# A fourth block unit in the second MLP's down projection, and an earlier first difference in the last stage

## The chip, the cores and the metric

The kernel runs on one core of one Trainium2 chip. The metric is the device time of one execution in microseconds (us): the median of three runs. A profile of one more execution gives the trace that the text reads.

## What is computed

Two layers of a causal decoder trunk over 512 tokens of width 1024, all in float32. Each layer is a mixer (layer 0: windowed attention beside a short convolution; layer 1: gated linear attention), a gated MLP with a width-3 convolution, and a gated per-layer embedding. The change lies in the last two pieces of layer 1:

```python
def _conv_ffn(h, w_up, conv_w, conv_b, w_down):
    u = _causal_depthwise_conv(h @ w_up, conv_w) + conv_b
    gate, up = jnp.split(u, 2, axis=-1)
    return (jax.nn.gelu(gate, approximate=False) * up) @ w_down       # 512x2816 @ 2816x1024

def _per_layer_embedding(x, p_i, norm, w_gate, w_proj):
    gate = jax.nn.sigmoid(_rms_norm(x, norm) @ w_gate)                # 512x1024 @ 1024x1024
    return gate * (p_i @ w_proj)                                      # 512x256  @ 256x1024
...
        x = x + _conv_ffn(_rms_norm(x, ffn_norm[i]), ...)
        x = x + _per_layer_embedding(x, p[i], ...)
```

## The kernel before

**Numbers in halves.** Every float32 operand of a large matmul is split into a rounded high half (written by ScalarE, ACT) and the rest (a subtraction on VectorE, DVE). A product is then three matmuls on TensorE (PE): high x high, high x low, low x high (`mm3`, L162 to L164). x lies transposed in SBUF as eight feature tiles `xT[0]` to `xT[7]`, each 128 features x 512 tokens.

**Seven block products.** Some matrix products are cut into 2 x 2 blocks and done by seven products of half-size blocks in place of eight (a Strassen-Winograd scheme). The function `seven` is a generator: it issues the products of 256 columns (L879 to L881), yields between groups of them so that the caller can put plain matmuls of 512 columns in between, and copies partial sums between PSUM banks on ACT (L890, L891, L900, L904). `first_forms`, `more_forms` and `cut_blocks` make the sums and differences of the weight blocks on DVE (L850, L851, L858, L861) and split them (L826 on ACT, L827 on DVE).

**The down stage** (`down`, one for each of the two MLPs, `i` = 0 and 1). The 1024 output features are four units `u` of two tiles each; the 2816 rows of the weight are three groups: B (rows of tiles 0 to 7), A (8 to 13), C (14 to 21). `plan` lists the steps in the order in which PE takes them: (unit, group, first row tile, last row tile, and for some steps the unit whose C rows are done by seven block products between the row tiles of this step). A plain row tile of a step is six matmuls of 512 columns. In the first MLP (`i == 0`) all four units have their C rows done by blocks (`blocked` is 4). In the second (`i == 1`) units 0 to 2 have, and unit 3's C rows are two plain steps, `(3, "C", 0, 4)` and `(3, "C", 4, 8)`. `loads` and `inner` list the weight blocks in the order of their loads: through the two buffers `raw` (L1135), or, for `inner`, into two tiles `zt` (L1144). `todo` and `pump` issue the cuts and sums a few steps ahead; `settled` adds a finished unit into x (L1193, and L1256 for the shared seventh part) and calls `finish` for its two tiles, once no block unit is left and the unit's last part is in.

**Finishing a tile in the second MLP** (`blocks`, L293 to L312): scale by the norm's gain into a scratch tile from the same pool of two `zt` tiles (`half`), split into halves (`split`, L109 and L110), sums and differences of 256 columns for the last stage's own block scheme (L308 to L312), and squares summed into `acc` (L284, L285). `e1` is the part of an even tile's first 256 tokens; `s1`, `s2`, ... are block sums.

**The last stage** (`ple1`). The 1024 x 1024 gate weight is four blocks b11, b12, b21, b22 of 512 x 512. `add` runs the products of one x form with one weight form (L1482 to L1484), `chunk` splits half a block (L1461 on ACT, L1462 on DVE) into `wh`/`wl` buffers (three each) or into a `four` tile (seven in the pool), `minus` is a difference of blocks (L1471). The first products are `e1` with b11; then `s1` with b12 - b11, the norm's merge (`end_norm`, transposes of `acc`, L329), the transposes of p (`load_p`, L1287), and so on. At the end x is turned back and written out.

**What sets the order.** A scheduler orders each engine's instructions by priority (`high_priority`), except where `manual_schedule` fixes the program order for the named engines: PE in `down`, and PE, DVE and ACT in `ple1`. Each engine takes its queue in order; loads are issued in order by SyncE (SP), and a load whose buffer is not free holds up the loads behind it.

Of the kernel before, what the change touches and what calls it, by code (L numbers as in the profile page):

```python
# [56 lines left out]
class Kernel:  # L57
# [46 lines left out]
    def split(self, hl, src, gain=None):  # L104

        nc = self.nc
        h, l = hl
        if gain is None:
            nc.scalar.activation(h, src, AF.Copy)  # L109
            nc.vector.tensor_tensor(l, src, h.bitcast(F32), ALU.subtract)  # L110
        else:
            nc.scalar.activation(h, src, AF.Copy, scale=gain)
            nc.vector.scalar_tensor_tensor(
                out=l, in0=src, scalar=gain, in1=h.bitcast(F32), op0=ALU.mult, op1=ALU.subtract
            )

    def weights(self, src, na, nb, by="b"):
        raw = self.raw(na, nb)
# [168 lines left out]
    def blocks(self, m, gain, scratch, tags):  # L287


        nc = self.nc  # L290
        H = S // 2
        gx = scratch()
        nc.scalar.activation(gx, self.xT[m], AF.Copy, scale=gain[:, m : m + 1])  # L293

        def parts(x):
            w = x.shape[1]
            h, l = self.pair(self.fp, *tags)
            self.split((h[:, :w], l[:, :w]), x)
            return lambda b, c: (h[:, b * H + c * P : b * H + (c + 1) * P], l[:, b * H + c * P : b * H + (c + 1) * P])

        if m % 2 == 0:
            self.even = gx
            self.e1 = parts(gx[:, :H])
        else:
            e, o = self.even, gx
            op = parts(o)
            s12, s34 = scratch(), scratch()
            nc.vector.tensor_tensor(s12[:, :H], e[:, H:], o[:, H:], ALU.add)  # L308
            nc.vector.tensor_tensor(s12[:, H:], s12[:, :H], e[:, :H], ALU.subtract)
            s12p = parts(s12)  # L310
            nc.vector.tensor_tensor(s34[:, :H], e[:, :H], e[:, H:], ALU.subtract)
            nc.vector.tensor_tensor(s34[:, H:], o[:, :H], s12[:, H:], ALU.subtract)  # L312
            s34p = parts(s34)
            e1 = self.e1
            at = lambda f, b: lambda c: f(b, c)
            self.forms.append(
                dict(e1=at(e1, 0), o1=at(op, 0), o2=at(op, 1), s1=at(s12p, 0), s2=at(s12p, 1), s3=at(s34p, 0),
                     s4=at(s34p, 1))
            )
        self.squares(m)  # L320
# [779 lines left out]
    def down(self, i, acts, forms, both, work, finish):  # L1100
# [7 lines left out]
        plan = [(0, "B", 0, 4), (0, "B", 4, 8), (0, "A", 0, 3), (0, "A", 3, 6)]  # L1108
        plan += [(1, "A", 0, 3), (1, "A", 3, 6), (1, "B", 0, 4), (1, "B", 4, 8, 0)]
        plan += [(2, "B", 0, 4, 1), (2, "B", 4, 8, 2)]  # L1110
        if i == 0:
            plan += [(2, "A", 0, 4, 3), (2, "A", 4, 6), (3, "B", 0, 4), (3, "B", 4, 8), (3, "A", 0, 3), (3, "A", 3, 6)]
            loads = ["B0", "A0", "A1", "B1", "C0", "B2", "C2", "A2", "B3", "A3"]
            inner = ["C1", "C3"]
        else:
            plan += [(2, "A", 0, 3), (2, "A", 3, 6), (3, "B", 0, 4), (3, "B", 4, 8)]
            plan += [(3, "C", 0, 4), (3, "C", 4, 8), (3, "A", 0, 3), (3, "A", 3, 6)]
            loads = ["B0", "A0", "A1", "B1", "C0", "B2", "C2", "A2", "B3", "C3", "A3"]
            inner = ["C1"]
        blocked = 4 - i  # L1120
        plan = [p if len(p) == 5 else p + (None,) for p in plan]
        got, cuts, gens, pending = {}, {}, {}, []

# [76 lines left out]
        with tc.manual_schedule(engines={ET.PE}):  # L1200
# [4 lines left out]
            for t, (u, name, k0, k1, s) in enumerate(plan):  # L1205
# [1 line left out]
                if own:  # L1207
                    banks[u] = [self.ps(), self.ps()]
                ends = t + 1 == len(plan) or plan[t + 1][0] != u
                joined = i == 0 and u == 3  # L1210

                def steps(lo, hi):
                    for k in range(lo, hi):
# [17 lines left out]
                if s is None:  # L1231
                    steps(0, k1 - k0)
                    settled(ends)
                    pump(1)
                    pend()
                    if work:
                        work.pop(0)()
                        if not work:
                            load_inner(inner.pop(0))
                else:  # L1240
                    g = gens[s]
                    steps(0, 1)
# [12 lines left out]
                    x = self.xT[2 * s + 1].rearrange("p (u t) -> p u t", u=2)  # L1255
                    nc.vector.tensor_tensor(x, x, V.unsqueeze(1).to_broadcast([P, 2, H]), ALU.add)  # L1256
                    if i == 0 and s == 3:
                        banks[3] = [X, Y]
                    else:
                        add(2 * s, X)  # L1260
                        add(2 * s + 1, Y)
                    pend()
                    due[s] -= 1
                    block_left -= 1
                    settled(False)
# [5 lines left out]
            self.nc.sync.dma_start(pin[e], src[:, :, e * P : (e + 1) * P])  # L1271
        return pin

    def load_p(self, i, pool, pin=None):

        nc = self.nc
        given = pin is not None
# [6 lines left out]
        for e in range(2):  # L1284
            ps = self.pa()
            for t in range(NT):
                nc.tensor.transpose(ps[:, t * P : (t + 1) * P], pin[e][:, t, :], self.ident)  # L1287
            hl = (four[:, 2 * e], four[:, 2 * e + 1]) if given else self.pair(pool, f"ph{e}", f"pl{e}")
            self.split(hl, ps)
            out.append(hl)  # L1290
        return out

    def ple0(self, fp):

# [141 lines left out]
    def ple1(self, fp):  # L1436
# [15 lines left out]
        count = [0]  # L1452

        def chunk(src):
            if count[0] % 6 < 3:
                h, l = (self.wide(g).rearrange("p (a b) -> p a b", b=H) for g in ("wh", "wl"))
            else:
                four = self.four(fp)
                h, l = four[:, :2], four[:, 2:]
# [70 lines left out]

        b11 = block(0, 0, True)
        w11 = chunks(b11)
        b12 = block(0, 1, True)
        pin = self.p_halves(1)
        b22 = block(1, 1, False)
        wj_raw = self.four(fp, F32)
        proj_load(1)
        b21 = block(1, 0, False)
        proj_load(0)
        with tc.high_priority(offset=150):  # L1540
            minus(b11, b12, b11)
            wt1 = [chunk(b11[:, :2, :])]
        X, Q = [[self.ps() for _ in range(2)] for _ in range(2)]
        both = (0, H)
        with tc.manual_schedule(engines={ET.PE, ET.DVE, ET.Activation}):
            add(X, "e1", w11, first=True)
            wt1.append(chunk(b11[:, 2:, :]))
            minus(b11, b22, b11)
            steps = [(j, i, both, Q[i]) for j in range(J) for i in range(2)]
            add(None, "s1", wt1, first=True, order=steps[:2])  # L1550

            self.end_norm()
            ka = [self.sp.tile([P, S], F32, tag="acc", name=self.nm("keep"), bufs=1), self.sq()]
            for k, x in zip(ka, X):
                nc.scalar.copy(k, x)
            wt2 = chunks(b11)
            pT = self.load_p(1, fp, pin)
            add(None, "s1", wt1, order=steps[2:])
            minus(b12, b22, b12, (0,))
            wj = chunk(wj_raw[:, 2:, :])  # L1560
            kd = keep(Q, "R")
# [521 lines left out]
```

## Time and profile before

| | us |
|---|---|
| three runs: median (lowest to highest) | 1204.29 (1204.18 to 1205.54) |
| the profiled execution's own time | 1203.80 |
| its span, from the first to the last instruction | 1202.0 |
| PE busy | 1194.0 |
| DVE busy | 989.3 |
| ACT busy | 681.1 |
| GpSimd busy | 43.7 |

A row of the timeline gives the start in us from the span's start, the duration, the engine, the line of the kernel, the operation, output<-input by the program's names and the shape. What stands in brackets at its end is the idle time of the engine just before and who ended it. The duration of a matmul includes its way through the array, which overlaps the next ones; the time that a matmul costs is the distance from its start to the next one's. A row of the windows view gives the stretch, its length, and the busy time of PE, weight loads (PEld), DVE, ACT and GpSimd (POOL), the granted clock of PE, the share of the DMA engines and GB/s. A row of the DMA view gives the tile and the tensor, the queue, the count, the size and the us from issue to landing. The granted clock of PE is 1.00 in every stretch.

### The profile page before, as it was taken

To read this page: it belongs to the slowest core of one execution; us is meant where nothing else is said; L and a number is where in the kernel's file an instruction comes from. 1 tells how busy PE (TensorE), PEld (TensorE's weight loads), DVE (VectorE), ACT (ScalarE), POOL (GpSimd) and SP (SyncE) were. 2 spreads that over 40 slices of the span, in tenths; PEclk is the share of its full clock that TensorE was granted. 3 is DMA by queue.
4 is the path that set the end of the run, shared out by engine and by line. 5 is a ranking of instruction groups with operands and counts; after the bars stand their busy time and mean duration, and the time that the engine had idled before them with its cause. 6 is when DMAs were issued, how large, how long until landed. Compare 5 with 4: busy or idle time off the path is not lost.

```text
span 1202.0 us, 17888 instructions
## 1 busy us (share of the span) xinstructions
PE 1194.0 (99%) x7085; PEld 1037.6 (86%) x7085; DVE 989.3 (82%) x1563; ACT 681.1 (57%) x1109; POOL 43.7 (4%) x64
## 2 busy tenths in 40 slices
PE   9999999999999999999999999999999999999998
PEld 8877788999899889888988988889999999888887
DVE  6786587899999996789769876677999999978595
ACT  7466465656555744566563555565555656645374
POOL 2600000000000000000100000000000000000000
PEclk9999999999999999999999999999999999999999
DMA  7221322323233342232422222313242423322501
GB/s 222 90 88 39 97 79 70 129 83 119 92 104 107 107 139 97 97 106 63 140 66 69 71 71 70 106 54 122 71 140 71 139 72 128 127 88 97 210 1 70
DMA packets 110839, 117.61 MB, mean 98 GB/s; under 512 B 2808, under 2 KB 105778, under 8 KB 110756
## 3 DMA queue, kind: packets, MB, share of 16 engines
q1 hardware_dynamic: 109920, 115.88, 29.7%
q8 instruction: 55, 0.90, 0.3%
q0 software_dynamic: 560, 0.42, 0.3%
q10 hardware_dynamic: 276, 0.18, 0.1%
q14 instruction: 28, 0.23, 0.1%
HBM read 114.37 MB, written 2.10 MB: 97 GB/s over the span
## 4 chain that ended last, share of the span: by engine, by line
PE 89%; DVE 6%; ACT 2%; issue 1%; POOL 1%; DMA 0%; SPq 0%; DVEq 0%; ACTq 0%; POOLq 0%
PE ps L162 11%; PE ps L163 11%; PE ps L164 11%; PE pa L163 7%; PE pa L162 7%; PE pa L164 7%; PE ps L879 6%; PE ps L881 6%; PE ps L880 6%; PE pa L879 2%; PE pa L881 2%; PE pa L880 2%; DVE wl L143 1%; PE ps L1484 1%; PE ps L1483 1%
## 5 line engine op out<-in xcount | busy, mean ns | idle before, releaser
L142 ACT ACTIVATE wh<-raw 128x1024 fp32r<-128x1024 f32 (+4 forms) x146 | 145.8, 999 | 124.5 <-PE ps L163 78.8
L143 DVE TENSOR_TENSOR wl<-raw,wh 128x1024 fp32r<-128x1024 f32 (+4 forms) x146 | 168.1, 1151 | 40.7 <-ACT wh L142 39.9
L826 ACT ACTIVATE wh<-raw 128x1024 fp32r<-128x1024 f32 x84 | 89.2, 1062 | 120.6 <-DVE raw L851 65.1
L939 DVE SCALAR_TENSOR_TENSOR zt<-z,vfa,zt 128x510 f32<-128x510 f32 (+1 forms) x176 | 130.6, 744 | 5.3 <-ACT zt L937 4.7
L827 DVE TENSOR_TENSOR wl<-raw,wh 128x1024 fp32r<-128x1024 f32 x84 | 102.6, 1221 | 21.3 <-ACT wh L826 21.2
L937 ACT ACTIVATE zt<-z,vfb 128x512 f32<-128x512 f32 x88 | 71.0, 810 | 21.5 <-DVE four L990 8.3
L162 PE MATMUL ps<-b,wh 128*128 128x512 f32 x192 | 76.8, 400 | 0.0
L163 PE MATMUL ps<-b,wh 128*128 128x512 f32 x192 | 75.1, 391 | 0.0
L164 PE MATMUL ps<-b,wl 128*128 128x512 f32 x192 | 75.0, 391 | 0.0
L879 PE MATMUL ps<-four,wh 128*128 128x256 f32 x248 | 69.4, 280 | 0.7 <-ACT ps L904 0.7
L163 PE MATMUL pa<-a,wh 128*128 128x512 f32 x176 | 69.0, 392 | 0.0
L163 PE MATMUL pa<-b,wh 128*128 128x512 f32 x176 | 69.0, 392 | 0.0
L162 PE MATMUL pa<-a,wh 128*128 128x512 f32 x176 | 69.0, 392 | 0.0
L162 PE MATMUL pa<-b,wh 128*128 128x512 f32 x176 | 69.0, 392 | 0.0
L881 PE MATMUL ps<-four,wl 128*128 128x256 f32 x248 | 68.8, 277 | 0.0
L880 PE MATMUL ps<-four,wh 128*128 128x256 f32 x248 | 68.6, 277 | 0.0
L164 PE MATMUL pa<-a,wl 128*128 128x512 f32 x176 | 68.4, 389 | 0.0
L164 PE MATMUL pa<-b,wl 128*128 128x512 f32 x176 | 68.4, 389 | 0.0
L162 PE MATMUL ps<-a,wh 128*128 128x512 f32 x128 | 50.6, 395 | 0.0
L162 PE MATMUL ps<-uh,wh 128*128 128x512 f32 x128 | 50.3, 393 | 0.0
L163 PE MATMUL ps<-a,wh 128*128 128x512 f32 x128 | 50.2, 392 | 0.0
L163 PE MATMUL ps<-ul,wh 128*128 128x512 f32 x128 | 50.1, 391 | 0.0
(488 smaller groups left out, 3577.4 us busy)
## 6 DMA issues: line engine op xcount, KB each, us to landing
raw<-in_ffn_w_up_dram SPq DMA_DIRECT2D x44, 1024.0 KB, 5.0
raw<-in_ffn_w_down_dram SPq DMA_DIRECT2D x13, 1024.0 KB, 4.8
raw<-in_hy_w_in_dram SPq DMA_DIRECT2D x8, 1024.0 KB, 5.1
raw<-in_gla_w_in_dram SPq DMA_DIRECT2D x8, 1024.0 KB, 5.2
raw<-in_ffn_w_down_dram SPq DMA_DIRECT2D x8, 768.0 KB, 4.2
raw<-in_ple_w_gate_dram SPq DMA_DIRECT2D x6, 1024.0 KB, 4.8
raw<-in_hy_w_out_dram SPq DMA_DIRECT2D x16, 256.0 KB, 4.0
raw<-in_gla_w_out_dram SPq DMA_DIRECT2D x4, 1024.0 KB, 4.8
```

The costliest lines, as they stand in the source:

```text
L142: nc.scalar.activation(hv, v, AF.Copy)
L143: nc.vector.tensor_tensor(lv, v, hv.bitcast(F32), ALU.subtract)
L162: mm(out, lh, rh, start=start, stop=False, **kw)
L163: mm(out, lh, rl, start=False, stop=False, **kw)
L164: mm(out, ll, rh, start=False, stop=stop, **kw)
L826: nc.scalar.activation(h, src, AF.Copy)
L827: nc.vector.tensor_tensor(l, src, h.bitcast(F32), ALU.subtract)
L879: mm(out, wh, xh, start=first and j == 0, stop=False, **kw)
L880: mm(out, wh, xl, start=False, stop=False, **kw)
L881: mm(out, wl, xh, start=False, stop=j == ND // 2 - 1, **kw)
L937: nc.scalar.activation(y, z, AF.Identity, scale=w2[:, f : f + 1], bias=bb[:, f : f + 1])
L939: nc.vector.scalar_tensor_tensor(out=y[:, tap:], in0=z[:, : S - tap], scalar=w[:, f : f + 1], in1=y[:, tap:], op0=ALU.mult, op1=ALU.add,)
```

## The change

In the second MLP the plan, the loads and `blocked` become those of the first: unit 3's C rows are done by seven block products within the step `(2, "A", 0, 4, 3)`, their weight block is loaded in two parts into `zt` tiles, and the two PSUM banks of that product are the ones into which unit 3's B and A rows are then summed. Unit 3 now ends with the A rows as before, but without the two plain C steps.

In the last stage:

- b12 is loaded into a `four` tile and b21 into a `raw` buffer (before: the other way round), so b12's load does not wait for a `raw` buffer.
- The first difference b12 - b11 is made in two halves with the split of the first half between them. The split of the second half is held (`issue_after`) behind the split of `e1` of x's seventh tile (`xT[6]`).
- `chunk` gives the third split a `four` tile and the fourth a `wh`/`wl` pair (before: the other way round).
- Within the `s1` products, the transposes of p and the split of the first half of the next form (`wt2`, the old difference taken from b22) come after two steps, then three more steps, then the norm's merge and the copies of `e1`'s sums, then the second half of `wt2` and the last three steps. The low halves of p (`rests`) follow after all of them. Before, the merge, the copies, both halves of `wt2` and p with its low halves all came after two steps.

```diff
@@ def split @@
-            nc.scalar.activation(h, src, AF.Copy)
-            nc.vector.tensor_tensor(l, src, h.bitcast(F32), ALU.subtract)
+            first = nc.scalar.activation(h, src, AF.Copy)
+            second = nc.vector.tensor_tensor(l, src, h.bitcast(F32), ALU.subtract)
...
+        return first, second
@@ def blocks @@
-            self.split((h[:, :w], l[:, :w]), x)
+            self.halves = self.split((h[:, :w], l[:, :w]), x)
...
             self.e1 = parts(gx[:, :H])
+            self.e1_split = self.halves
@@ def down @@
-        if i == 0:
-            plan += [(2, "A", 0, 4, 3), (2, "A", 4, 6), (3, "B", 0, 4), (3, "B", 4, 8), (3, "A", 0, 3), (3, "A", 3, 6)]
-            loads = ["B0", "A0", "A1", "B1", "C0", "B2", "C2", "A2", "B3", "A3"]
-            inner = ["C1", "C3"]
-        else:
-            plan += [(2, "A", 0, 3), (2, "A", 3, 6), (3, "B", 0, 4), (3, "B", 4, 8)]
-            plan += [(3, "C", 0, 4), (3, "C", 4, 8), (3, "A", 0, 3), (3, "A", 3, 6)]
-            loads = ["B0", "A0", "A1", "B1", "C0", "B2", "C2", "A2", "B3", "C3", "A3"]
-            inner = ["C1"]
-        blocked = 4 - i
+        plan += [(2, "A", 0, 4, 3), (2, "A", 4, 6), (3, "B", 0, 4), (3, "B", 4, 8), (3, "A", 0, 3), (3, "A", 3, 6)]
+        loads = ["B0", "A0", "A1", "B1", "C0", "B2", "C2", "A2", "B3", "A3"]
+        inner = ["C1", "C3"]
+        blocked = 4
...
-                joined = i == 0 and u == 3
+                joined = u == 3
...
-                    if i == 0 and s == 3:
+                    if s == 3:
                         banks[3] = [X, Y]
@@ def load_p @@
-            self.split(hl, ps)
-            out.append(hl)
-        return out
+            nc.scalar.activation(hl[0], ps, AF.Copy)
+            out.append((hl, ps))
+
+        def rests():
+            for (h, l), ps in out:
+                nc.vector.tensor_tensor(l, ps, h.bitcast(F32), ALU.subtract)
+
+        if not later:
+            rests()
+        hls = [hl for hl, _ in out]
+        return (hls, rests) if later else hls
@@ def ple1 @@
-            if count[0] % 6 < 3:
+            if count[0] % 6 < 3 and count[0] != 2 or count[0] == 3:
...
-        b12 = block(0, 1, True)
+        b12 = block(0, 1, False)
...
-        b21 = block(1, 0, False)
+        b21 = block(1, 0, True)
         proj_load(0)
+        rounded, rest = (x.ins for x in self.e1_split)
         with tc.high_priority(offset=150):
-            minus(b11, b12, b11)
+            minus(b11, b12, b11, (0,))
             wt1 = [chunk(b11[:, :2, :])]
+            minus(b11, b12, b11, (1,))
...
             add(X, "e1", w11, first=True)
-            wt1.append(chunk(b11[:, 2:, :]))
+            with tc.issue_after(rounded), tc.issue_after(rest):
+                wt1.append(chunk(b11[:, 2:, :]))
             minus(b11, b22, b11)
             steps = [(j, i, both, Q[i]) for j in range(J) for i in range(2)]
             add(None, "s1", wt1, first=True, order=steps[:2])
-
+            pT, rests = self.load_p(1, fp, pin, True)
+            wt2 = [chunk(b11[:, :2, :])]
+            add(None, "s1", wt1, order=steps[2:5])
             self.end_norm()
             ...
-            wt2 = chunks(b11)
-            pT = self.load_p(1, fp, pin)
-            add(None, "s1", wt1, order=steps[2:])
+            wt2.append(chunk(b11[:, 2:, :]))
+            add(None, "s1", wt1, order=steps[5:])
+            rests()
```

More of the change, by code (lines that the diff above doesn't have):

```diff
@@ L108, in split @@
         if gain is None:
-            nc.scalar.activation(h, src, AF.Copy)
-            nc.vector.tensor_tensor(l, src, h.bitcast(F32), ALU.subtract)
-        else:
-            nc.scalar.activation(h, src, AF.Copy, scale=gain)
-            nc.vector.scalar_tensor_tensor(
+            first = nc.scalar.activation(h, src, AF.Copy)
+            second = nc.vector.tensor_tensor(l, src, h.bitcast(F32), ALU.subtract)
+        else:
+            first = nc.scalar.activation(h, src, AF.Copy, scale=gain)
+            second = nc.vector.scalar_tensor_tensor(
                 out=l, in0=src, scalar=gain, in1=h.bitcast(F32), op0=ALU.mult, op1=ALU.subtract
             )
+        return first, second
     def weights(self, src, na, nb, by="b"):
@@ L1272, in p_halves, with load_p @@
         return pin
-    def load_p(self, i, pool, pin=None):
+    def load_p(self, i, pool, pin=None, later=False):
         nc = self.nc
```

## The prediction

> **What bounds the kernel now.** I read the page first: the share of each engine, then the chain that ended last.
>
> ```profile
> PE 1194.0 (99%) x7085; PEld 1037.6 (86%) x7085; DVE 989.3 (82%) x1563; ACT 681.1 (57%) x1109; POOL 43.7 (4%) x64
> ...
> PE 89%; DVE 6%; ACT 2%; issue 1%; POOL 1%; DMA 0%; SPq 0%; DVEq 0%; ACTq 0%; POOLq 0%
> ```
>
> TensorE (PE) is busy almost from end to end and the chain is made of it. A busy share says little, since matmuls overlap, so what counts is the distance from one matmul's start to the next in the timeline: where that distance is always the same, the queue of PE never runs dry, and only fewer or shorter matmuls save time. I therefore went through the timeline of PE from the second MLP's down stage to the end, looking for starts that come later than the beat. The first MLP's down stage serves as a natural experiment: it already takes all four units by seven block products, the second one only three. Here are the first matmul of each stage and the first after it:
>
> ```profile
> 408.77 0.40 PE L162 MATMUL ps<-uh,wh 128*128 128x512 f32 x1
> ...
> 524.69 0.39 PE L162 MATMUL ps<-a,wh 128*128 128x512 f32 x1
> ...
> 1026.37 0.40 PE L162 MATMUL ps<-uh,wh 128*128 128x512 f32 x1
> ...
> 1143.44 0.39 PE L1482 MATMUL ps<-wh,b 128*128 128x512 f32 x1
> ```
>
> The stage with four such units took 524.69 - 408.77 = 115.92 us, that with three 1143.44 - 1026.37 = 117.07 us. The matmul work is otherwise the same, so 1.15 us is the first estimate of what the fourth unit brings.
>
> **The change part by part.** *The fourth unit's C rows.* Removed are 48 matmuls of 512 columns (8 row tiles x 2 feature tiles x 3 products of halves); this is their place, from the first of them to the first of the next step:
>
> ```profile
> 1124.40 0.39 PE L162 MATMUL ps<-four,wh 128*128 128x512 f32 x1
> ...
> 1135.28 0.39 PE L162 MATMUL ps<-four,wh 128*128 128x512 f32 x1
> ```
>
> That is 10.88 us, or 0.2267 us each. Added are 84 of 256 columns (7 products x 4 x 3); the order of the changed kernel's PE queue indeed has 36 instructions more, so the change does what it says. Their price is in the first MLP, where the same 84 lie between the four plain steps of the unit before:
>
> ```profile
> 487.75 0.40 PE L162 MATMUL ps<-four,wh 128*128 128x512 f32 x1
> ...
> 489.14 0.28 PE L879 MATMUL pa<-four,wh 128*128 128x256 f32 x1
> ...
> 490.52 0.40 PE L162 MATMUL ps<-four,wh 128*128 128x512 f32 x1
> ...
> 502.90 0.40 PE L162 MATMUL ps<-four,wh 128*128 128x512 f32 x1
> ```
>
> The whole run of four steps and seven products took 502.90 - 487.75 = 15.15 us. The four steps are 24 matmuls of 512 columns, 24 x 0.2267 = 5.44 us, which leaves 9.71 us for the 84, their changes of width included. The first product alone, 12 matmuls, took 490.52 - 489.14 = 1.38 us, 0.115 us each, so nothing waited there. Against 10.88 us this saves 1.17 us, in line with the 1.15 us of the whole stages.
>
> A product of the seven can still wait for the copy or the split ahead of it. The three units of the second MLP show how much; this is the worst place of the third:
>
> ```profile
> 1102.11 0.39 PE L164 MATMUL ps<-uh,wl 128*128 128x512 f32 x1
> 1102.44 0.38 PE L879 MATMUL ps<-b,wh 128*128 128x256 f32 x1
> 1102.66 0.28 PE L880 MATMUL ps<-b,wh 128*128 128x256 f32 x1
> ```
>
> The starts are 0.33 and 0.22 us apart instead of 0.23 and 0.11: 0.21 us lost, because the norm's squares and splits stand ahead of the copy in ACT's queue. The change holds that norm work back until the fourth unit, so this loss can move there or vanish here. Bounds: from 0.21 us given back to 0.21 us gained beside the 1.17. I take zero, nearest to the first MLP's fourth unit, which lost nothing.
>
> *What this adds elsewhere.* In blocks the unit needs on DVE eight operations of 512 and two of 1024 elements a row, in place of two of 1024; on ACT four copies of 256, three splits of 512 and two of 1024, in place of two of 1024. The paces of DVE, start to start, are in four neighbouring rows:
>
> ```profile
> 1106.47 0.42 DVE L110 TENSOR_TENSOR b<-zt,b 128x256 fp32r<-128x256 f32 x1
> 1106.81 1.22 DVE L143 TENSOR_TENSOR wl<-raw,wh 128x1024 fp32r<-128x1024 f32 x1
> 1107.95 0.68 DVE L110 TENSOR_TENSOR b<-zt,b 128x512 fp32r<-128x512 f32 x1
> 1108.55 0.42 DVE L308 TENSOR_TENSOR zt<-zt 128x256 f32<-128x256 f32 x1
> ```
>
> So 0.34 us for 256, 1.14 for 1024, 0.60 for 512, and DVE gets 8 x 0.60 = 4.8 us more. It has room in the stretch from the third unit's end to the last stage:
>
> ```profile
> 1106.60:1143.44 36.84, 36.84 (x164) 30.50 (x163) 21.79 (x31) 13.51 (x20) 0.00 (x0) 1.00 0.56 196
> ```
>
> Columns two to five are PE, weight loads, DVE and ACT: DVE is busy for 21.79 of 36.84 us. Cost: nothing on the path, as long as DVE's work keeps its order of need. If that cover is gone, each us by which DVE is late is a us of PE.
>
> *The norm's blocks come later.* The two scratch tiles that carry the fourth unit's rows are also the norm's scratch, and units 0 to 2 are finished only once no block unit is left. Before, 168 matmuls, 38 us of plain steps, lay behind that point; after, 2.72 + 10.88 + 8.16 = 21.8 us (12, 48 and 36 matmuls at 0.2267). DVE's last split for the unit, in the first MLP:
>
> ```profile
> 495.88 1.22 DVE L827 TENSOR_TENSOR wl<-zt,wh 128x1024 fp32r<-128x1024 f32 x1 [1.71 <-ACT wh L826]
> ```
>
> It ended 497.10 - 487.75 = 9.35 us into the 15.15. So from that split to the last stage PE has 15.15 - 9.35 + 21.76 = 27.6 us. In the changed kernel's DVE order I count between the two 15 operations of 256, 17 of 512, two of 768 and seven of 1024. With the 768s bounded by a 1024 this is 15 x 0.34 + 17 x 0.60 + 9 x 1.14 = 25.6 us. It fits with 2 us to spare, and the last two of them (2.3 us) are needed only some steps into the last stage. This is the thinnest cover of the change.
>
> *The last stage.* Nothing is added to or taken from PE; the eight transposes of p and the four of the norm's merge only swap places with matmuls. Moved are the first weights' difference (its first half now ahead of x's last sums) and one split behind the first norm split of x's sixth tile. What these free is seen here, first who delivers, then who needs it:
>
> ```profile
> 1146.52 0.42 DVE L110 TENSOR_TENSOR a<-zt,a 128x256 fp32r<-128x256 f32 x1
> ...
> 1149.07 0.68 DVE L285 TENSOR_TENSOR acc<-acc,sq 128x512 f32<-128x512 f32 x1
> ```
>
> ```profile
> 1147.97 0.39 PE L1484 MATMUL ps<-wh,a 128*128 128x512 f32 x1
> ...
> 1150.24 0.60 PE L329 MATMUL pa<-cf,acc 128*128 128x128 f32 x4
> ```
>
> The split ends 1146.94, 1.03 us ahead of its matmul; the sum of squares 1149.75, 0.49 us ahead of the merge. Both were already in time. Moving the merge three steps (3 x 0.68) back makes the second margin larger than 2.5 us, but a margin that grows brings no time. Gain: zero; cost: zero while the other margins stay above zero.
>
> *The loads.* The order on SP's queue changes: b12's block now goes to a tile that PE frees with the last product of the fourth unit, and b11's (the first one needed), b22, the projection, b21 and p's second half stand behind it.
>
> ```profile
> raw<-in_ple_w_gate_dram SPq DMA_DIRECT2D x2, 1024.0 KB, 5.4
> four<-in_ple_w_gate_dram SPq DMA_DIRECT2D x2, 1024.0 KB, 4.9
> ```
>
> ```profile
> 1135.25 1.06 ACT L1461 ACTIVATE wh<-raw 128x1024 fp32r<-128x1024 f32 x1 [4.59 <-PE ps L163]
> ```
>
> Even one after the other, b12 and b11 land 4.9 + 5.4 = 10.3 us after that product; the first cut of b11 waits, as in the row above, for PE to give back a weight buffer, which happens 2.72 + 10.88 = 13.6 us after it. PE still ends that wait, with 3.3 us to spare. b21 and p's second half wait for the last cut of the A rows, for which PE frees a weight buffer half-way through the B rows, 8.16 + 5.44 = 13.6 us before the last stage; if DVE's queue delays that cut by 5 us, 8 us are left, and p's half is needed 6.8 us into the stage.
>
> The sum: -1.17 +- 0.21 from the products, 0 from the rest; I take -1.15, the whole-stage comparison. Against the profiled execution that is 1203.80 - 1.15 = 1202.65 us. The median of the runs, 1204.29, lies 0.49 above it, so 1204.29 - 1.15 = 1203.1 us. What a measurement of this kernel can tell from no change is about 0.2%, 2.4 us; the forecast of -0.1% lies inside it.
>
> **The rivals.** *DVE becomes the bound.* The 25.6 us of DVE work in 27.6 us leave no room for handshakes with ACT, and each one costs. From 2.0 us of waits on (4.3 us, if the last two operations slip behind), PE stands at the last stage's first weights. With 6 us of waits in the window, PE loses about 4, and the time is 1204.29 - 1.15 + 4 = 1207.1 us. For it: that stretch has long waits of DVE for ACT, like the 1.71 us in the row of 495.88. Against: the wait there is for PE to free a buffer, before the window. I give it 0.10.
>
> *The gain is given back.* One stall of about 1.2 us in the last stage, where splits of the later weights are made just in time, and the time stays at 1204.3 us. The 0.49 us margin shows that such places exist, but it is the one that widens. 0.07.
>
> *Half-wide matmuls are bound by their weight loads.* If 84 pairs go at the mean of a weight load, 1037.6/7085 = 0.146 us, they take 12.3 us in place of 10.88, and the time is 1204.29 + 1.4 = 1205.7 us. The 0.115 us of the first MLP's product speaks against it. The Trainium skill has this rule ("TensorE: Matmul & The Clock Gate", Back-to-back issue gap): in a stream of weight load and matmul pairs both set the spacing, about 81 ns at 128 and 131 ns at 512 columns; a line between them would make 84 x 0.098 - 48 x 0.131 = +1.9 us, an estimate. This trace does not agree: 0.2267 us at 512 columns. 0.02.
>
> *More than the sum.* The small losses at the products of all four units close as the norm work leaves their queue (three times 0.2 to 0.3), and the restarts in the last stage shorten a little: some 1.2 us more, 1201.9 us, and 1201.8 with the 0.11 us by which the lowest of the three runs lies under the median. This is at the line of 0.2%, and I count it as faster. No row shows those restarts to depend on the moved work. 0.11.
>
> **How the numbers follow.** The forecast keeps 0.70. Its own range is 1202.7 to 1203.5 (the 0.21 either way and rounding). The range of 8 in 10 takes in "more" at the low end, 1201.8, and no gain at the high end with the 1.25 us by which the highest of the three runs lay above the median: 1204.3 + 1.25 = 1205.6; outside is the DVE case. Faster by over 0.2%: 0.11. Slower by over 0.2%: 0.10. Within: 0.70 + 0.07 + 0.02 = 0.79.
>
> **What would show it right or wrong.** Right: the second down stage takes 115.9 us like the first, its 84 new matmuls start 0.113 to 0.118 us apart, and the last stage from its first matmul to the end is as long as before. DVE's window behind the fourth unit would be nearly full, with no PE start off the beat at the first weights of the last stage. Wrong: a wait of PE for a split of L1462's line there (DVE is the bound), a first cut of b11 that a DMA releases, or starts 0.14 us apart in the new products.

## The result and the profile after

The changed kernel took 1203.07 us (median of 21 runs, 1202.1 to 1204.92), the kernel before 1204.61 (median of 21, 1203.98 to 1206.14). The ratio is 0.9987, with a 95% interval of 0.9981 to 0.9993: it is faster, by 0.07% to 0.19%, less than the 0.2% that the forecast took as its line. The profiled execution took 1202.58 us with a span of 1200.8 (before 1203.80 and 1202.0).

The page of the changed kernel, its busy times:

```profile
PE 1192.9 (99%) x7121; PEld 1038.1 (86%) x7121; DVE 994.2 (83%) x1571; ACT 685.2 (57%) x1116; POOL 42.9 (4%) x64
```

PE has 36 matmuls more and is busy 1.1 us less; DVE has 4.9 us more. PE remains the bound. Lines have moved: the plain matmuls are now L163 to L165, those of the products L881 to L883, those of the last stage L1486 to L1488, the merge L331.

The timeline of PE at the starts of the second down stage, of the fourth unit's step, of the step behind it and of the last stage, and the last matmul of all:

```profile
1026.32 0.40 PE L163 MATMUL ps<-uh,wh 128*128 128x512 f32 x1
...
1105.30 0.40 PE L163 MATMUL ps<-four,wh 128*128 128x512 f32 x1
...
1120.45 0.40 PE L163 MATMUL ps<-four,wh 128*128 128x512 f32 x1
...
1142.24 0.39 PE L1486 MATMUL ps<-wh,b 128*128 128x512 f32 x1
...
1196.22 0.28 PE L1488 MATMUL ps<-four,a 128*128 128x256 f32 x1
```

The stage takes 1142.24 - 1026.32 = 115.92 us, which was 117.07. The fourth unit's step takes 1120.45 - 1105.30 = 15.15 us, the same as in the first MLP. The last stage runs as long as before: 53.98 us to its last matmul (before 53.95). All of the gain that the traces show lies in the down stage. They are one execution each, with 1.2 us between their spans; the medians differ by 1.54 us, and the interval allows 0.8 to 2.3.

In the windows view, DVE's stretch from its last split for the fourth unit to the last stage (columns: length, PE, PEld, DVE, ACT, POOL, clock, DMA share, GB/s):

```profile
1114.61:1142.24 27.63, 27.63 (x142) 23.50 (x141) 25.17 (x41) 18.27 (x29) 0.00 (x0) 1.00 0.65 229
```

DVE is busy for 25.17 of 27.63 us, PE for all of it.

### The profile page after: what moved, and what is told of

It is laid out like the page before. It is cut to its first block, busy times and chain, and to the rows that moved or that the text cites. A ratio compares the mean times of both kernels' runs of the same rounds, so it can differ in the third digit from the quotient of the medians.

```text
span 1200.8 us, 17976 instructions
## 1 busy us (share of the span) xinstructions
PE 1192.9 (99%) x7121; PEld 1038.1 (86%) x7121; DVE 994.2 (83%) x1571; ACT 685.2 (57%) x1116; POOL 42.9 (4%) x64
## 4 chain that ended last, share of the span: by engine, by line
PE 89%; DVE 6%; ACT 2%; issue 1%; POOL 1%; DMA 0%; SPq 0%; ACTq 0%; DVEq 0%; POOLq 0%
PE ps L163 11%; PE ps L164 11%; PE ps L165 11%; PE pa L163 7%; PE pa L164 7%; PE pa L165 7%; PE ps L881 6%; PE ps L883 6%; PE ps L882 6%; PE pa L881 2%; PE pa L883 2%; PE pa L882 2%; DVE wl L144 1%; PE ps L1488 1%; PE ps L1486 1%
## 5 line engine op out<-in xcount | busy, mean ns | idle before, releaser
L143 ACT ACTIVATE wh<-raw 128x1024 fp32r<-128x1024 f32 (+4 forms) x144 | 143.7, 998 | 114.3 <-PE ps L164 64.7
L163 PE MATMUL ps<-b,wh 128*128 128x512 f32 x192 | 76.7, 400 | 0.0
L165 PE MATMUL ps<-b,wl 128*128 128x512 f32 x192 | 75.0, 391 | 0.0
L881 PE MATMUL ps<-four,wh 128*128 128x256 f32 x256 | 71.6, 280 | 0.7 <-ACT ps L906 0.7
L883 PE MATMUL ps<-four,wl 128*128 128x256 f32 x256 | 71.0, 277 | 0.0
L882 PE MATMUL ps<-four,wh 128*128 128x256 f32 x256 | 70.8, 277 | 0.0
L163 PE MATMUL pa<-a,wh 128*128 128x512 f32 x176 | 69.0, 392 | 0.0
L163 PE MATMUL pa<-b,wh 128*128 128x512 f32 x176 | 69.0, 392 | 0.0
L165 PE MATMUL pa<-a,wl 128*128 128x512 f32 x176 | 68.4, 389 | 0.0
L165 PE MATMUL pa<-b,wl 128*128 128x512 f32 x176 | 68.4, 389 | 0.0
L881 PEld LDWEIGHTS ps<-four,wh 128*128 128x128 f32 x256 | 48.0, 188 | 3.2 <-ACT ps L906 1.6
L163 PE MATMUL ps<-a,wh 128*128 128x512 f32 x128 | 50.6, 395 | 0.0
L163 PE MATMUL ps<-uh,wh 128*128 128x512 f32 x128 | 50.3, 393 | 0.0
```

What stands on the lines that cost most here:

```text
L143: nc.scalar.activation(hv, v, AF.Copy)
L163: mm(out, lh, rh, start=start, stop=False, **kw)
L165: mm(out, ll, rh, start=False, stop=stop, **kw)
L881: mm(out, wh, xh, start=first and j == 0, stop=False, **kw)
L882: mm(out, wh, xl, start=False, stop=False, **kw)
L883: mm(out, wl, xh, start=False, stop=j == ND // 2 - 1, **kw)
```

## The experiments

The stages of all kernels, from the timelines: the first matmul of the second down stage, the first and the last matmul of the last stage, and the differences, in us. (The 58.56 us that some expectations give for the last stage includes 4.6 us from the last matmul to the end of the span. In experiment 12 the first matmul of the last stage stands among the A rows of unit 3, so that its two stages can't be told apart. The ratios below are those of the runs, with a 95% interval in brackets; they differ from the quotient of the two medians by up to 0.04%.)

| kernel | down starts | last stage starts | last matmul | down | last | both |
|---|---|---|---|---|---|---|
| before | 1026.37 | 1143.44 | 1197.39 | 117.07 | 53.95 | 171.02 |
| changed | 1026.32 | 1142.24 | 1196.22 | 115.92 | 53.98 | 169.90 |
| 1: products alone | 1026.06 | 1141.95 | 1197.35 | 115.89 | 55.40 | 171.29 |
| 2: last stage alone | 1026.09 | 1143.20 | 1197.19 | 117.11 | 53.99 | 171.10 |
| 3: products and load | 1026.37 | 1142.27 | 1196.22 | 115.90 | 53.95 | 169.85 |
| 4: changed, late load | 1026.49 | 1142.46 | 1197.29 | 115.97 | 54.83 | 170.80 |
| 5: changed, early merge | 1028.17 | 1144.13 | 1198.08 | 115.96 | 53.95 | 169.91 |
| 6: half-wide plain steps | 1026.29 | 1144.07 | 1198.02 | 117.78 | 53.95 | 171.73 |
| 7: copy first, all units | 1025.86 | 1142.38 | 1196.37 | 116.52 | 53.99 | 170.51 |
| 8: copy first, third unit | 1026.19 | 1142.41 | 1196.39 | 116.22 | 53.98 | 170.20 |
| 9: copy first, first MLP | 1026.54 | 1142.53 | 1196.52 | 115.99 | 53.99 | 169.98 |
| 10: eight idle sums | 1026.87 | 1143.48 | 1197.47 | 116.61 | 53.99 | 170.60 |
| 11: the same on 3 | 1027.39 | 1143.90 | 1197.84 | 116.51 | 53.94 | 170.45 |
| 12: sixteen idle sums | 1026.36 | | 1206.27 | | | 179.91 |

### 1. The products alone

`down` as changed, `ple1` as before:

```diff
+        plan += [(2, "A", 0, 4, 3), (2, "A", 4, 6), (3, "B", 0, 4), ...]     # for both MLPs
+        blocked = 4
         b12 = block(0, 1, True)
         b21 = block(1, 0, False)
         minus(b11, b12, b11)
```

> Only the fourth down unit goes by seven products; the last stage keeps its old order. Theory (the gain comes from the products alone, and the moves of the last stage are worth nothing): the down stage takes 115.92 us as in the changed kernel, the last stage 58.56 us as before, the time is 1.15 us under the kernel before (0.9990). Rival (the moves of the last stage keep the gain): DVE has 4.8 us more ahead of the norm's last sums, whose margin before was 0.49 us; the merge then waits, the last stage takes 59.2 to 60.0 us, and the time is within 0.5 us of the kernel before (0.9996 to 1.0002).

Measured: 1204.12 us against 1203.91, ratio 0.9999 (0.9990 to 1.0008). The down stage has its gain, and the last stage takes 1.45 us longer than before. The rival was right in its numbers; the rows show a wait for a load behind them. The timeline of PE at the merge, of DVE ahead of it, and of SP's queue:

```profile
1148.54 0.39 PE L1478 MATMUL ps<-wh,b 128*128 128x512 f32 x1
1150.11 0.66 PE L329 MATMUL pa<-cf,acc 128*128 128x128 f32 x4 [1.17 <-DVE acc L285]
```

```profile
1132.65 0.95 DVE L143 TENSOR_TENSOR wl<-raw,wh 128x768 fp32r<-128x768 f32 x1
...
1138.74 1.23 DVE L1465 TENSOR_TENSOR raw<-raw,raw 128x1024 f32<-128x1024 f32 x1 [2.66 <-DMA raw<-in_ple_w_gate_dram]
...
1149.37 0.68 DVE L285 TENSOR_TENSOR acc<-acc,sq 128x512 f32<-128x512 f32 x1
```

```profile
1133.67 0.37 SPq L1443 DMA_DIRECT2D raw<-in_ple_w_gate_dram  x1
```

The same split on DVE and the same load on SP's queue in the kernel before:

```profile
1130.69 0.96 DVE L143 TENSOR_TENSOR wl<-raw,wh 128x768 fp32r<-128x768 f32 x1 [4.48 <-ACT wh L142]
```

```profile
1131.68 0.37 SPq L1449 DMA_DIRECT2D raw<-in_ple_w_gate_dram  x1
```

Read from the load on, in the run of experiment 1: b12's load needs a `raw` buffer, and is issued at 1133.67, 0.07 us after DVE's split of the down stage's last weights out of that buffer ends (1132.65 + 0.95). DVE then stands for 2.66 us in front of the first difference until the block has landed. Behind that wait it still has the differences, splits and sums of x that lead up to the last sum of squares, which ends at 1150.05. PE, which could have begun the merge 0.23 us after 1148.54, stands until 1150.11: 1.34 us lost. Before the change the same load was issued at 1131.68, 11.8 us ahead of the last stage; here it is 8.3 us ahead, because, counted from the start of the down stage, the last stage begins 1.2 us sooner while the buffer comes free 2.3 us later. In the kernel before, DVE had stood idle for 4.48 us in front of that split; here it comes to it straight from three splits of the norm's blocks, so it is DVE's fuller queue that gives the buffer back late.

### 2. The last stage alone

`ple1` as changed, `down` as before.

> Only the last stage is reordered; the fourth down unit stays in plain steps. Theory and rival agree that nothing is gained where DVE has no more to do: the down stage takes 117.07 us, the last stage 58.4 to 58.6 us, ratio 0.9998 to 1.0002. A third theory, that the moved first weights' difference saves PE time of its own, would give a last stage of 58.3 us or less and a ratio under 0.9998.

Measured: 1204.60 us against 1203.91, ratio 1.0002 (0.9993 to 1.0010), last stage 53.99 us. The moves save nothing by themselves. Together with the first experiment: one half alone brings 0, the other half alone brings 0, both bring 1.1 us.

### 3. The products and, of the moves, only the load

```diff
-        b12 = block(0, 1, True)
+        b12 = block(0, 1, False)
-        b21 = block(1, 0, False)
+        b21 = block(1, 0, True)
```

> The fourth unit by products with the old order of the last stage, as in the first experiment, and of the last stage's moves only the load: b12's block goes to the tile that the products free, b21's to the buffer that comes free late. Theory (the late load alone took the gain back): the load is issued near 1119.5 instead of 1133.67 us, DVE's wait of 2.66 us for it goes, the sum of squares is ready by 1148 and the merge finds it there: last stage 58.56 us, 1.15 us under the kernel before. Rival (DVE simply has too much to do ahead of the merge, in the old order): the merge still waits 0.3 to 1.2 us, last stage 58.9 to 59.8 us.

Measured: 1202.69 us against 1203.94, ratio 0.9989 (0.9980 to 0.9999); both stages together 169.85 us, as in the changed kernel (169.90). Two changed arguments carry the whole of what the last stage's moves are worth. In the timeline of SP, DVE and PE:

```profile
1119.66 0.37 SPq L1443 DMA_DIRECT2D four<-in_ple_w_gate_dram  x1
```

```profile
1147.90 0.69 DVE L285 TENSOR_TENSOR acc<-acc,sq 128x512 f32<-128x512 f32 x1
```

```profile
1149.08 0.60 PE L329 MATMUL pa<-cf,acc 128*128 128x128 f32 x4
```

The load is issued 14 us sooner, the sum of squares ends at 1148.59, and the merge finds it there with 0.49 us to spare, the margin that it had before.

### 4. The changed kernel with the late load

The reverse of the edit above, with halves, order and merge as changed.

> The changed kernel with b12's block in the buffer that comes free late again, and b21's in the early one; halves, merge and order stay as changed. Theory of the load: DVE waits about 2.7 us for the block in place of the 1.12 us there now, 1.5 us later, which is just over the 1.40 us margin of x's sixth split: 0.0 to 0.4 us lost there, and the moved merge hides the rest; last stage 58.6 to 59.0 us. Rival (the load is what matters, whatever the order): 59.5 us and more, the gain gone as in the first experiment.

Measured: 1203.00 us against 1203.94, ratio 0.9994 (0.9985 to 1.0003); the last stage takes 54.83 us, 0.85 more than the changed kernel. That is between the two expectations, and over the theory's 0.4. DVE waits for the load as in the first experiment:

```profile
1139.67 1.23 DVE L1475 TENSOR_TENSOR raw<-raw,raw 128x1024 f32<-128x1024 f32 x1 [3.07 <-DMA raw<-in_ple_w_gate_dram]
```

With the new order the merge is not hit, but the first splits of `xT[6]` now come late: starts of PE at 1146.68 and 1147.43, 0.36 and 0.42 us after the ones before. So the halves and the later merge are worth 55.40 - 54.83 = 0.57 us as long as the load is late, and nothing once it is early.

### 5. The changed kernel with the merge where it was

```diff
-            pT, rests = self.load_p(1, fp, pin, True)
-            wt2 = [chunk(b11[:, :2, :])]
-            add(None, "s1", wt1, order=steps[2:5])
             self.end_norm()
...
+            wt2 = chunks(b11)
+            pT = self.load_p(1, fp, pin)
+            add(None, "s1", wt1, order=steps[2:])
```

> The changed kernel with the norm's merge, p's transposes and the second weights' cut where they stood before (the load and the halves of the difference stay changed). Theory of the load: the merge needs the sum of squares at 1149 us at the earliest and it is ready at 1146.77, so nothing waits: last stage 58.5 to 58.7 us. Rival (the moved merge is what saves the gain): it waits 0.5 us or more, last stage 59.1 us or more.

Measured, one run: last stage 53.95 us; no wait at the merge. (Its time, 1204.44 us, includes 1.8 us lost ahead of everything that was edited: its first down stage already starts at 410.54, in the changed kernel at 408.72.) The moved merge isn't what keeps the gain.

### 6. Plain steps in half-wide matmuls

The kernel before, unit 3's C rows in 96 matmuls of 256 columns in place of 48 of 512:

```diff
+                                for z in (slice(0, H), slice(H, S)):
+                                    self.mm3(banks[u][c][:, z], cuts[t](...), (ah[:, z], al[:, z]), ...)
```

> The kernel before, with the fourth unit's C rows still in plain steps, but each of the 48 matmuls of 512 columns issued as two of 256: 96 of 256 columns and 96 weight loads. Theory (a matmul costs its columns): the steps go at 0.113 to 0.116 us a matmul, 10.9 to 11.1 us in all, 0 to 0.3 us more than before. Rival (half-wide matmuls are bound by their weight loads, 0.146 us each): 14.0 us in all, 3.1 us more, 1207.7 us.

Measured: 1204.67 us against 1203.91, ratio 1.0005 (0.9996 to 1.0014); the down stage takes 117.78 us, 0.71 longer than before. The timeline of PE, the first of the 96 and the first matmul behind them:

```profile
1124.37 0.28 PE L162 MATMUL ps<-four,wh 128*128 128x256 f32 x1
...
1135.88 0.40 PE L162 MATMUL ps<-four,wh 128*128 128x512 f32 x1
```

The 96 take 11.51 us in place of 10.88: 0.63 us more, not the 0 to 0.3 of the theory and far from the rival's 3.1. A half-wide matmul cost 11.51/96 = 0.120 us here and 9.71/84 = 0.1156 in the fourth unit's products; both are near half of 0.2267, so columns set the price, with 2% to 6% on top. The Trainium skill ("TensorE: Matmul & The Clock Gate", Back-to-back issue gap) would have made this edit dearer by 96 x 0.098 - 48 x 0.131 = 3.1 us, an estimate on the line between its 81 and 131 ns. This trace does not agree. Why the plain steps pay 0.004 us more than the products wasn't found.

### 7. The copy ahead of the weight cut

In the changed kernel the third unit still has its small loss at the seventh product, though the norm's squares are no longer in that queue. The timelines of PE and of ACT:

```profile
1102.12 0.39 PE L165 MATMUL ps<-uh,wl 128*128 128x512 f32 x1
1102.47 0.38 PE L881 MATMUL ps<-b,wh 128*128 128x256 f32 x1
1102.70 0.28 PE L882 MATMUL ps<-b,wh 128*128 128x256 f32 x1
```

```profile
1101.09 1.06 ACT L143 ACTIVATE wh<-raw 128x1024 fp32r<-128x1024 f32 x1 [2.34 <-PE ps L882]
1102.06 0.36 ACT L906 COPY ps<-ps 128x256 f32<-128x256 f32 x1
```

The starts of PE are again 0.35 and 0.23 us apart. The copy that the product needs (L906) stands behind a cut of the next weights (L143), which itself has waited 2.34 us for PE to free a weight buffer. The experiment turns the two round:

```diff
-                    cut_done(s)
-                    pump(1)
+                    with tc.issue_after(self.turned_over.ins):
+                        cut_done(s)
+                        pump(1)
```

> The changed kernel, with the last cut of a unit's weights (ACT's rounding, which waits for PE to free a weight buffer) and the norm work of that place put behind the copy that the seventh product needs, in both MLPs. Theory (the 0.24 us lost at that copy in units 1 to 3 of each MLP comes from the cut that stands ahead of it in ACT's queue, not from the norm's squares as was forecast): the starts behind the copy go back to 0.11 and 0.23 us apart, six times 0.2 us are gained, 1.2 us, unless the later cut is then late for the last two products, which gives back 0.4 to 0.5 us in each unit and makes it slower by up to 2 us. Rival (the norm's squares are what delays the copy): units 1 to 3 of the second MLP keep their 0.24 us where squares still stand ahead.

Measured: 1203.44 us against 1203.91, ratio 0.9994 (0.9985 to 1.0003); the second down stage takes 116.52 us, 0.60 longer. The late starts at the copies of units 1 to 3 are gone, so the cut was the cause, but three waits stand in the timeline of PE, of which the first was a smaller loss in the changed kernel (0.23 us) and the others are new:

```profile
1074.82 0.50 PE L163 MATMUL ps<-uh,wh 128*128 128x512 f32 x1 [0.32 <-DVE xT L1189]
...
1094.09 0.39 PE L883 MATMUL pa<-b,wl 128*128 128x256 f32 x1 [0.17 <-DVE wl L829]
...
1117.76 0.38 PE L881 MATMUL ps<-b,wh 128*128 128x256 f32 x1 [0.21 <-ACT ps L906]
```

What the copies gain comes back at these places, and more; the copy of the fourth unit, which lost nothing in the changed kernel, is late now.

### 8 and 9. The copy first in the third unit, in both MLPs and in the first alone

The same edit under `s == 2`, then under `i == 0 and s == 2`.

> The changed kernel, with the copy put ahead of the weight cut in ACT's queue in the third unit of each MLP alone. Theory (the cut, which waits for PE to free a weight buffer, is what holds the copy up, and only units in which nothing needs that cut at once can gain): the two late starts behind the copy vanish in that unit, 0.24 us in each MLP, 0.1 to 0.5 us in all, under what the time can show (ratio 0.998 to 1.000 of the kernel before). Rival (as with all four units, what is gained comes back at a later copy or split): each down stage stays at 115.9 to 116.1 us.

> The changed kernel, with the copy ahead of the weight cut in the third unit of the first MLP alone, where it gained 0.23 us and brought no later loss. Theory: the first down stage takes 115.73 us in place of 115.96, the second stays at 115.92, the last at 58.56; 0.23 us under the changed kernel, ratio to the kernel before 0.9985. Rival (the second MLP's order shifts with it and gives the gain back): the two stages together are as long as in the changed kernel, ratio 0.9987.

With both MLPs: 1202.86 us against 1203.49, ratio 0.9996 (0.9987 to 1.0006). The first down stage takes 524.54 - 408.81 = 115.73 us (changed kernel 524.68 - 408.72 = 115.96), as the theory wanted; the second takes 116.22, because its fourth unit's copy is late again: in this run, too, PE waits for it, 0.20 us ahead of a matmul at 1117.76. With the first MLP alone: 1202.64 us against 1203.94, ratio 0.9989 (0.9980 to 0.9998). Its first stage takes 524.87 - 409.14 = 115.73, its second 115.99: 0.15 us less than the changed kernel over both stages and the last one, too little for the times to show. No version was clearly faster than the changed kernel.

### 10 and 11. Idle work on DVE

```diff
+                    if i == 1 and s == 3:
+                        for _ in range(8):
+                            nc.vector.tensor_reduce(self.load, self.xT[7].rearrange("p (t d) -> p t d", d=P), op=ALU.add, axis=AX.X)
                     settled(False)
```

The first run adds this to the changed kernel, the second to that of experiment 3 (which the expectation calls the fifth).

> The changed kernel with eight idle sums over 512 elements (about 0.6 us each, 4.8 to 5.4 us together) added to DVE's queue behind the fourth unit's last sum, in the window whose slack was forecast as 2.0 us (4.3 if two operations slip). Theory from the changed kernel's trace: DVE has waits of 1.27 and 1.12 us there and 1.40 us of margin at x's sixth split, 3.8 us in all, so PE loses 1.0 to 1.6 us. By the forecast's count it loses 0.5 to 3.4 us. Rival (the queue of DVE is not near the bound): nothing lost.

> The kernel of the fifth experiment (products and the sooner load, the rest of the last stage as before) with the eight idle sums in DVE's window. Theory (halves of the difference and the later merge are a reserve: in the changed kernel the merge has 5.2 us to spare, here 0.49): the late DVE reaches the merge, which waits, and the loss is 0.3 to 1.5 us larger than the 0.69 us that the same load cost the changed kernel. Rival (the waits ahead of the last stage take up the delay, and the reserve isn't needed): 0.6 to 0.8 us as there.

Measured on the changed kernel, one run (1203.92 us): 0.70 us lost in 169.90, less than the 1.0 expected and at the low end of the forecast's count. The idle sums and the one late start of PE:

```profile
1112.41 2.13 DVE L1264 TENSOR_REDUCE mhalf<-xT 128x4 f32<-128x512 f32 x3
...
1134.64 0.95 DVE L144 TENSOR_TENSOR wl<-raw,wh 128x768 fp32r<-128x768 f32 x1
```

```profile
1135.65 0.50 PE L165 MATMUL ps<-four,wl 128*128 128x512 f32 x1 [0.30 <-DVE wl L144]
```

Three sums took 1114.46 - 1112.41 = 2.05 us, the other five 0.60 each: 5.05 us, of which 5.05 - 0.70 = 4.35 were free. PE waits for a split of unit 3's A rows, not in the last stage. Part of the free time lay further ahead: without the sums, DVE waits for ACT in front of its last split for the fourth unit, as the timeline of the changed kernel shows, and this wait took in about 1.6 of the first 2.05 us.

```profile
1113.38 1.23 DVE L829 TENSOR_TENSOR wl<-zt,wh 128x1024 fp32r<-128x1024 f32 x1 [1.66 <-ACT wh L828]
```

The added work also shifts the order of a few operations in DVE's queue, so 4.35 us is the slack of this order. On the kernel of experiment 3, in one run (1204.29 us), the same work cost 170.45 - 169.85 = 0.60 us, as the rival had it. So the halves and the late merge were no reserve that this load reached.

### 12. Twice as much idle work

> The changed kernel with sixteen idle sums in DVE's window in place of eight. Eight took 5.05 us of DVE (three at 0.685, five at 0.60) and cost PE 0.69 us, so 4.4 us were free. Theory (past the slack each us by which DVE is late is a us of PE, the price that the forecast put on its DVE rival): sixteen take 9.85 us, of which 5.5 us show: the down stage and the last one together are 5 to 6 us longer than in the changed kernel, 1208 us. Rival (the eight were absorbed in other ways, and there is more room further on): under 3.5 us.

Measured, one run: 1212.75 us, 10.0 us lost (179.91 against 169.90), where the theory had 5 to 6. First the timeline of PE around the large wait, then the windows view (the granted clock stands behind the five engines):

```profile
1146.97 0.39 PE L1490 MATMUL ps<-wh,a 128*128 128x512 f32 x1
1152.61 0.79 PE L1491 MATMUL ps<-wl,a 128*128 128x512 f32 x1 [5.25 <-DVE wl L1470]
1153.20 0.63 PE L1492 MATMUL ps<-wh,a 128*128 128x512 f32 x1
...
1157.47 0.63 PE L1490 MATMUL ps<-four,b 128*128 128x512 f32 x1
```

```profile
1146.97:1152.60 5.63, 0.39 (x2) 0.00 (x0) 5.60 (x12) 2.84 (x5) 0.00 (x0) 0.87 0.00 0
1152.60:1158.10 5.50, 5.49 (x13) 4.33 (x14) 4.32 (x4) 1.06 (x1) 0.00 (x0) 0.51 0.00 0
1158.10:1163.00 4.90, 4.90 (x29) 4.12 (x29) 1.60 (x3) 2.37 (x4) 0.00 (x0) 1.00 0.00 0
```

The large wait is 5.41 us (1152.61 - 1146.97 less one beat of 0.23). Another 1.84 us are lost around unit 3's A rows, 0.63 of them ahead of the last stage's first matmul, which waits for ACT there, and most of the rest for DVE: 7.25 in all. Another 2.6 us come after the large wait: 13 matmuls from 1152.61 take 5.56 us in place of 2.95, most of them 0.427 us apart, at a granted clock of 0.51.

But this is not the queue of the changed kernel with more work in it: its order differs. The large wait is for the split of b11's second half. The timeline of DVE in this run:

```profile
1144.29 1.28 DVE L1190 TENSOR_TENSOR xT<-xT,ps 128x512 f32<-128x512 f32 x2
1145.49 1.23 DVE L1470 TENSOR_TENSOR four<-raw,four 128x1024 fp32r<-128x1024 f32 x1
...
1151.34 1.22 DVE L1470 TENSOR_TENSOR wl<-raw,wh 128x1024 fp32r<-128x1024 f32 x1
```

And in the changed kernel:

```profile
1139.90 1.22 DVE L1466 TENSOR_TENSOR wl<-raw,wh 128x1024 fp32r<-128x1024 f32 x1
...
1142.29 1.28 DVE L1189 TENSOR_TENSOR xT<-xT,ps 128x512 f32<-128x512 f32 x2
```

There the split stands ahead of x's last sums (the rows `xT<-xT,ps`). Here it stands behind them and behind ten more operations of the norm (in the gap of the fence, from 1146.64 on), 1.2 + 4.7 = 5.9 us of work. In its old place it would have ended near 1151.34 + 1.22 - 5.9 = 1146.7 us, ahead of the 1147.2 at which PE wanted it. By this estimate the large wait, and with it the slow stretch, comes from the order and not from the amount of work, so the run doesn't show what a us of lateness costs.

## Why the prediction was right, and where its steps were not

The time is right: 1203.1 forecast, 1203.07 measured, and inside 0.2% of the kernel before, as forecast. That the two meet to 0.03 us is luck in part: the kernel before measured 1204.61 this time, 0.32 more than the median that the forecast started from, and the medians differ by 1.54 us and not by 1.15. The gain between the traces, 1.12 us over the two stages, is the better test, and it agrees. Step by step:

**The products** were right to the hundredth. The stage takes 115.92 us as in the first MLP, and the 84 matmuls cost 15.15 - 5.44 = 9.71 us.

**The +-0.21 us** had the wrong cause. It was put down to the norm's squares and splits. In the changed kernel they have left that queue and the loss stays; experiments 7 to 9 show the cut that stands ahead of the copy. The loss neither moved nor vanished, so taking zero was right for a reason that was not.

**DVE's added work and its window** were right in size: 4.9 us more on the page (forecast 4.8), 25.17 us of work in 27.63 (25.6 in 27.6). The slack of 2.0 us, or 4.3 if two operations slip, was 4.35 under experiment 10's load. That this meets the larger number is chance: about 1.6 us of it lay in a wait of DVE ahead of the forecast's window, and what came late was a split of the A rows and not the first weights. The price of the DVE rival, a us of PE for each us of lateness, stays open: experiment 12 lost 10.0 us, but with another order of DVE's queue.

**The last stage** is the step that failed. "Gain: zero" and "a margin that grows brings no time" were read from the margins of the kernel before, and held there (experiment 2). But once the products were in, the 1.03 us shrank to 0.18 (experiment 1: that split ends at 1146.31, its matmul starts at 1146.49) and the 0.49 us was gone: the products alone make the last stage 1.45 us longer. The path that the forecast left out runs through a buffer: DVE's added work was to cost "nothing on the path", but it gives a `raw` buffer back later, b12's load waits for that buffer, and the difference, splits and sums behind the load come late for the merge. Of the moves the sooner load of b12 is worth all of these 1.45 us, the others nothing beside it. The forecast followed that load only to see that it came in time, not to price what it replaced. So the sum should have read -1.18 (products), +1.45 (last stage left as it was), -1.45 (load), not -1.15 and zero. The total came out because the change held the load together with the products, not because the last stage had nothing to lose.

**The rivals.** "The gain is given back" is what the first experiment did, at the very place with 0.49 us of margin that the forecast named and dismissed as the one that widens: its 1204.3 us was no gain, and the products alone gave none (ratio 0.9999). Weight loads as the bound are refuted at their 0.146 us by experiment 6. "More than the sum" needed the small losses to close, which stayed. Of the loads, PE and not a DMA released b11's first cut, as forecast. In the timeline of ACT:

```profile
1134.05 1.06 ACT L1465 ACTIVATE wh<-raw 128x1024 fp32r<-128x1024 f32 x1 [2.09 <-PE ps L164]
```

## What to carry to other kernels

When a change shortens a stage, go through every load, buffer and queue whose work is due at the start of the next one, and subtract the gain from its margin: a margin below the gain gives the gain back. Price each part of a change in the presence of the others: a part that is worth nothing alone can be what keeps another's gain. Put a late operation down to the row that stands just ahead of it in its engine's queue, not to other work known to lie there. When idle work is added to find a slack, compare the order of the queues with and without it before the loss is read as a price.

## What the runs showed of the hardware

PE's clock fell after a single wait of 5.25 us: the next 5.5 us ran at a granted 0.51, matmuls of 512 columns 0.427 us apart in place of 0.2267, which cost 2.6 us beyond the wait. The waits of 1.17 us in experiment 1 and 0.82 us in experiment 12 were not followed by a slow stretch: the starts from 1151.70 and from 1136.93 on are 0.23 us apart again. The Trainium skill says this ("TensorE: Matmul & The Clock Gate", What's actually happening): after an idle window of about 3.4 us the array runs at half its clock until it has been busy for about as long again. The trace agrees with the fall to half the clock; its slow stretch, 5.5 us in this one case, is longer than the page's figure.
